# Heads 78 and 79 stored by GpSimd in four DMAs of 5, 4, 116 and 3 rows

## The chip, the cores and the metric

The kernel runs on one core of a Trainium2 chip. The metric is the device time of one execution in microseconds (us). The kernel before took 133.29, 133.81 and 133.81 us in three runs, a median of 133.81 us; a fourth run, the profiled one, took 133.37 us.

The core has a TensorE (PE) for matrix products, a VectorE (DVE), a ScalarE (ACT) and a GpSimd (POOL) for elementwise work, and a SyncE (SP) that only issues transfers. Transfers between the chip's main memory and the core's own memory are run by sixteen DMA engines. GpSimd, SyncE and ScalarE each have a queue of their own to them: q0, q1 and q10 in the profile.

## The reference

```python
B, H, S, D = 8, 12, 512, 64
mask[i, j] = 1 if j == i or j is an ancestor of i in the binary heap tree, else 0
scores = einsum('bhqd,bhkd->bhqk', Q, K) / sqrt(D) + (1 - mask) * (-1e9)
weights = softmax(scores, axis=-1)
out = einsum('bhqk,bhkd->bhqd', weights, V)        # float32
```

So there are 96 heads of 512 tokens with 64 numbers each. A token attends only to itself and to the nodes above it in the tree. The inputs are float32, 12.58 MB each, and so is the output.

## The kernel before, in words

**Layout.** The 96 heads are worked off in 48 pairs, `i = 0` to 47 (`NP` = 48). On the core a head of the output is a block of 128 partitions with 256 float32 numbers each: partition `p` holds tokens `4p` to `4p + 3`, which in main memory is one unbroken row of 1 KB. Eight heads share a tile `of` of 128 x 8 x 4 x 64 (`ofs[j]`, L695), from a pool of eleven, so that no tile of results has to be reused early.

**A pair.** `scores1` and `scores2` multiply queries and keys on TensorE and take the exponential on ScalarE; the mask enters as a second, short product. `values` (L650) multiplies the weights with V, with a column of ones that yields the sums; `norm` (L692) divides on VectorE, a reciprocal at L699 and a product at L701, and writes the head into `of`.

**Loads and stores.** All loads of Q, K and V but the first few are issued by GpSimd, in the order of one list that `pool_program` (L725) writes out by hand. The list also holds copies that GpSimd makes itself. `pool(i)` (L843) is called once per pair and takes operations from the head of the list as long as `ready` (L773) lets them; for a store that is `i >= 4 * (h0 // 8 + 1)`, when all heads of the tile have been issued to VectorE. Operations are never overtaken, so a DMA that waits on GpSimd holds back all that follow.

**The stores.** `store` (L708) writes `n` heads from `h0`, and partitions `p0` to `p1` of them, in one DMA. The main loop puts them on three queues:

- GpSimd (at the end of `pool_program`, L763 to L770) stores tiles of eight heads each, heads 0 to 71 and 80 to 87, a DMA of 1 MB each, and in between heads 74 to 79, a DMA of 768 KB. The last three entries of its list that move output are heads 64 to 71, 74 to 79 and 80 to 87.
- SyncE stores heads 72 and 73 in `store_apart` (L719), after pair 38: for each of the two heads one DMA of partitions 0 to 115 and one of partitions 116 to 127.
- SyncE also stores the heads of the last four pairs: 88 and 92 in one DMA, then 89, 93, 90, 94 and 91 in one of 128 KB each (L898 to L903); ScalarE issues head 95 (L904).

The GpSimd list ends with copies (`lay_beside`, L440) that rearrange the last tiles of queries and keys; two of them stand between heads 64 to 71 and heads 74 to 79.

**Semaphores.** The DMAs that GpSimd issues take eight semaphores in turn. A DMA whose semaphore is still that of an earlier one waits for the earlier one's landing before it is issued. Such waits are written by the framework and not in the kernel's text.

Of the kernel before, what the change touches and what calls it, by code (L numbers as in the profile page):

```python
# [119 lines left out]
def kernel(  # L120
# [7 lines left out]
    nc = tc.nc  # L128
    B, H, S, D = Q.shape
    P = nc.NUM_PARTITIONS  # L130
# [6 lines left out]
    KB, VB = 8, 16  # L137
# [577 lines left out]


    APART, APART_AT, APART_ROWS = 72, 38, 116

    def store_apart():  # L719

        for p0, p1 in ((0, APART_ROWS), (APART_ROWS, P)):
            for h in range(2):
                store(nc.sync, APART + h, 1, 1, p0, p1)

    def pool_program():  # L725

        ops = [
            (load_k, 2, 2), (load_q, 2, 2), (load_v, 0, 4), (load_v, 4, 4),
            (load_k, 4, 2), (load_k, 6, 2), (load_q, 4, 2), (load_k, 8, 4),
            (load_q, 6, 2), (load_q, 8, 4), (load_v, 8, 8), (load_k, 12, 4),  # L730
            (load_q, 12, 4), (load_k, 16, 4), (load_rows, 1, "upper"),
            (load_q, 16, 4), (load_rows, 1, "even"), (load_k, 20, 4), (load_rows, 1, "odd"),
            (load_q, 20, 4), (load_k, 24, 8), (load_q, 24, 4), (load_rows, 2, "upper"),
            (load_q, 28, 4), (load_rows, 2, "leaves0", "leaves1"), (load_k, 32, 8), (load_q, 32, 8),
            (load_rows, 3, "upper"),
            (spread_pool, (1, "Z0", 8, 16), (1, "Z1", 8, 16), (1, 6, 8, 16), (1, 9, 8, 16)),
            (load_q, 40, 8), (load_k, 40, 8), (load_rows, 3, "leaves0", "leaves1"), (load_q, 48, 8),
            (spread_top, 2), (spread_pool, (2, "Z0", 0, 16), (2, "Z1", 0, 16)), (load_k, 48, 8),
            (spread_pool, (2, "X", 0, 16), (2, "M", 0, 16), (2, "D1", 0, 16)), (spread_top, 3, 0, 12),
            (load_rows, 4, "upper"), (spread_top, 3, 12, 16),  # L740
        ]
        loaded, stored = 72, 0
        for h in range(56, NH, KB):
            top = [(spread_top, h // VB + 0)] if h % VB == 8 and 4 <= h // VB + 0 < NH // VB else []
            if top:
                top.append((spread_pool, (h // VB, "Z0", 0, 16), (h // VB, "Z1", 0, 16)))
            ops += [(load_q, h, KB)] + top + [(load_k, h, KB)]
            if h == 64:
                ops.append((
                    spread_pool, *[(3, part, 0, 16) for part in ("Z0", "Z1", "X", "M", "D1")]  # L750
                ))
            while loaded < min(h + 32, NH):
                names = ("leaves0", "leaves1") if loaded % VB else ("upper",)
                ops.append((load_rows, loaded // VB) + names)
                loaded += KB
            if top:
                o = h // VB
                ops.append((spread_pool, *[(o, part, 0, 16) for part in ("X", "M", "D1")]))
            if stored + KB + BEHIND <= h + KB:
                ops.append((store, nc.gpsimd, stored, KB))  # L760
                stored += KB
        ops.insert(-1, (lay_beside, "qst", 80 // KB))
        while stored < NH - KB:  # L763
            n = 2 if stored == APART else 0
            ops.append((store, nc.gpsimd, stored + n, KB - n))
            if stored == 40:
                ops.append((lay_beside, "kst", 80 // KB))
            if stored == 64:
                ops += [(lay_beside, "qst", 88 // KB), (lay_beside, "kst", 88 // KB)]
            stored += KB  # L770
        return ops
# [58 lines left out]
    def spread_by(copy, table, steady, i):  # L830
# [7 lines left out]
        for args in todo:  # L838
            spread(copy, *args)

    program = pool_program()

    def pool(i):  # L843
# [91 lines left out]
```

## Time and profile before

| | us |
|---|---|
| median of 3 runs | 133.81 |
| lowest and highest | 133.29, 133.81 |
| the profiled execution, its time | 133.37 |
| its span in the profile | 131.6 |
| granted TensorE clock, mean | 0.975 |

The span is from the first instruction to the last; what lies between the span and the time of the same execution, 1.8 us, is start and end of the program outside it. "Windows" are stretches of the span with the busy time of each engine in them, the granted clock, the share of time that the sixteen DMA engines were busy (1.00 is all sixteen, and a little over 1 occurs because packets overlap) and the bytes that they moved. The DMA view of a window has the same share in 40 slices, in tenths, the GB/s of each slice, and the packets of each queue (packets, MB, share). A timeline row has the start, the busy time, the engine, the line and the operation, and in brackets the idle time ahead of it and what ended it. "Landing" is the time from the issue of a DMA to the last of its semaphore's increments.

### The profile page before, as it was taken

The page shows a single profiled execution, that of the slowest core. Times are in us where ns is not written, and L with a number is a line of the kernel's source. Part 1 is how long each engine was busy: PE and PEld are TensorE (multiplying, and loading weights), DVE is VectorE, ACT ScalarE, POOL GpSimd, SP SyncE. Part 2 cuts the span into 40 slices and gives each one's busy share as a digit, 9 for nine tenths or more (in the row PEclk, how much of TensorE's full clock was granted, in tenths as well). Part 3 has the DMA queues.
Part 4 walks back from the last instruction along what each step waited for, and adds up shares of the span by engine and source line. Part 5 has one row for each costly group of instructions (what it writes and reads, how often), then busy time and mean ns, then how long its engine had stood idle before and what let it go on. Part 6 is the DMA issues. An engine that isn't in the chain of part 4 may idle for free.

```text
span 131.6 us, 5430 instructions
## 1 busy us (share of the span) xinstructions
PE 114.2 (87%) x2350; PEld 79.7 (61%) x2353; DVE 104.3 (79%) x254; ACT 101.1 (77%) x163; POOL 83.2 (63%) x114
## 2 busy tenths in 40 slices
PE   6985999999899897899999897896999999999800
PEld 2451676667567566677677674675676777666500
DVE  3528769988999998989899889898799977973620
ACT  4358289989799995968998788796799789899700
POOL 6988726245493999995399899944999945002000
PEclk9998599999999999999999999999999999999995
DMA  4999999999999999999999999999999999999992
GB/s 118 230 176 194 196 199 204 197 205 203 201 204 208 207 207 205 208 207 203 207 207 201 306 270 205 285 291 234 339 218 333 240 291 399 399 402 399 389 342 72
DMA packets 27959, 32.25 MB, mean 245 GB/s; under 512 B 1208, under 2 KB 23096, under 8 KB 27936
## 3 DMA queue, kind: packets, MB, share of 16 engines
q0 software_dynamic: 25760, 29.89, 111.4%
q1 hardware_dynamic: 1616, 1.57, 3.5%
q10 hardware_dynamic: 560, 0.46, 1.2%
q8 instruction: 18, 0.29, 0.8%
q14 instruction: 5, 0.04, 0.1%
HBM read 37.94 MB, written 12.58 MB: 384 GB/s over the span
## 4 chain that ended last, share of the span: by engine, by line
PE 34%; DVE 25%; DMA 16%; ACT 8%; POOL 7%; issue 5%; ACTq 0%; POOLq 0%
PE ob L662 12%; DMA kst<-in_K_dram 11%; DVE of L701 8%; DVE vt L371 6%; DMA qst<-in_Q_dram 5%; ACT e L618 4%; PE s L567 4%; POOL vt L371 3%; ACT e L584 3%; PE s L574 3%; DVE rec L699 2%; PE s L601 2%; PE ktp L477 2%; DVE kq L486 2%; PE s L612 2%
## 5 line engine op out<-in xcount | busy, mean ns | idle before, releaser
L584 ACT ACTIVATE e<-s 128x1024 bf16<-128x1024 f32 x40 | 40.9, 1022 | 13.0 <-PE s L574 12.5
L662 PE MATMUL ob<-vt,e 128*128 128x65 bf16 (+1 forms) x940 | 37.6, 198 | 1.6 <-DVE of L701 1.2
L662 PEld LDWEIGHTS <-e 128*128 128x128 bf16 (+1 forms) x960 | 30.5, 103 | 9.9 <-PE s L612 1.3
L371 POOL COPY vt<-vst 32x512 int32<-32x512 int32 (+4 forms) x44 | 32.5, 739 | 4.8 <-PE ob L662 2.6
L618 ACT ACTIVATE e<-s 128x384 bf16<-128x384 f32 x80 | 34.7, 491 | 0.0
L701 DVE TENSOR_TENSOR of<-ob,rec 128x512 f32<-128x512 f32 x47 | 32.5, 692 | 1.6
L371 DVE COPY vt<-vst 32x1024 bf16<-32x1024 bf16 (+5 forms) x47 | 22.0, 467 | 2.4 <-DMA vst<-in_V_dram 1.6
L699 DVE RECIPROCAL rec<-ob 128x8 f32<-128x8 f32 x47 | 9.6, 205 | 11.1 <-PE ob L662 9.7
L574 PE MATMUL s<-qq,kq 64*128 64x512 bf16 x80 | 15.3, 377 | 0.0
L709 POOL DMA_DIRECT2D out_dram<-of x11 | 9.8, 895 | 8.5 <-DVE of L701 8.0
L612 PE MATMUL s<-qq,kq 64*128 64x160 bf16 (+1 forms) x320 | 14.9, 208 | 0.1
L612 PEld LDWEIGHTS <-kq 64*128 64x128 bf16 x320 | 12.4, 94 | 4.2 <-issue 0.3
L601 PEld LDWEIGHTS <-codes 40*128 40x128 bf16 x80 | 6.4, 95 | 10.5 <-issue 4.9
L567 PE MATMUL s<-far,codes 40*128 40x512 bf16 x64 | 12.5, 386 | 0.1
L254 POOL DMA_DIRECT2D qst<-in_Q_dram x12 | 8.5, 704 | 5.6 <-DMA kst<-in_K_dram 2.9
L543 DVE COPY qq<-qtp 128x1024 bf16<-128x1024 bf16 x16 | 10.9, 683 | 1.0 <-PE qtp L538 1.0
L580 ACT ACTIVATE e<-s 128x1024 bf16<-128x1024 f32 x8 | 8.2, 1022 | 4.6 <-PE s L574 4.6
L371 ACT COPY vt<-vst 32x512 int32<-32x512 int32 (+3 forms) x19 | 10.4, 545 | 1.4 <-DMA vst<-in_V_dram 1.0
L601 PE MATMUL s<-far,codes 40*128 40x384 bf16 x64 | 10.6, 324 | 0.6 <-ACT e L618 0.5
L254 POOL DMA_DIRECT2D kst<-in_K_dram x11 | 8.5, 775 | 4.1 <-DMA vst<-in_V_dram 1.8
L477 PE MATMUL ktp<-ptile,kst 128*64 128x128 bf16 x256 | 9.9, 220 | 0.9 <-DMA kst<-in_K_dram 0.6
L538 PE MATMUL qtp<-ptile,qst 128*64 128x128 bf16 x192 | 7.4, 220 | 2.9 <-DMA qst<-in_Q_dram 2.0
(56 smaller groups left out, 155.3 us busy)
## 6 DMA issues: line engine op xcount, KB each, us to landing
out_dram<-of POOLq DMA_DIRECT2D x10, 1024.0 KB, 15.4
kst<-in_K_dram POOLq DMA_DIRECT2D x9, 512.0 KB, 14.3
qst<-in_Q_dram POOLq DMA_DIRECT2D x8, 512.0 KB, 16.2
vst<-in_V_dram POOLq DMA_DIRECT2D x12, 256.0 KB, 13.7
vst<-in_V_dram POOLq DMA_DIRECT2D x6, 512.0 KB, 12.7
qst<-in_Q_dram POOLq DMA_DIRECT2D x6, 256.0 KB, 12.4
kst<-in_K_dram POOLq DMA_DIRECT2D x4, 256.0 KB, 9.7
out_dram<-of POOLq DMA_DIRECT2D x1, 768.0 KB, 14.7
```

The costliest lines, as they stand in the source:

```text
L254: return nc.gpsimd.dma_start(out=kept[b][:, h0 % KB:h0 % KB + n, :, :].rearrange("p (g x) t d -> p g (x t d)", x=x), in_=src[:, h0 // x:(h ...
L371: return copy(out=dst, in_=src)
L477: nc.tensor.transpose(out=columns(kp[64 * a:64 * a + 64, :], mixed, *dims), in_=st[:, place[a], 4 * u + t, :], identity=ptile[:, 0:128],)
L567: nc.tensor.matmul(out=sp[:, a, :], lhsT=(k1code if i < WIDE else k1wide)[64 * a:64 * a + CODE_ROWS, :], rhs=(q1code, q1wide, q1far)[(i >= ...
L574: nc.tensor.matmul(out=sp[:, a, :], lhsT=keys(i, a, TOP), rhs=qTs[i][64 * a:64 * a + 64, :, :].rearrange("p t c -> p (t c)"), start=False, ...
L584: ) if i < WIDE else nc.scalar.activation(
L601: nc.tensor.matmul(out=flat[:, a, :, :].rearrange("p u (t c) -> p u t c", t=4)[:, :, :, 32 // n:], lhsT=k2wide[64 * a:64 * a + CODE_ROWS, ...
L612: nc.tensor.matmul(out=flat[:, a, :, lo:hi], lhsT=keys(i, a, WTILE2[t]), rhs=qT[64 * a:64 * a + 64, :, lo:hi], start=False, stop=t == 1, s ...
L618: nc.scalar.activation(out=e2s[i % NE][:, a, :, 32:128].rearrange("p t (r u) -> p t r u", u=n), in_=flat[:, a, :, :].rearrange("p u (t r) ...
L662: nc.tensor.matmul(out=ob[lo:hi, a, 65 * t:65 * t + 65], lhsT=e[:, a, PLACE[t], lo:hi], rhs=vt[vtile[tile_v][0]][:, head(i, a) % VB, vtile ...
L699: nc.vector.reciprocal(out=rec[:, a:a + n, :, :], in_=o4[:, a:a + n, :, D:D + 1])
L701: nc.vector.tensor_tensor(out=ofs[j][:, h0:h1 + 1:head(i, 1) - head(i, 0), :, :], in0=o4[:, a:a + n, :, 0:D], in1=rec[:, a:a + n, :, :].to ...
```

## The change

The list's entry for heads 74 to 79 becomes five entries: heads 74 to 77 over all partitions, and heads 78 and 79 over partitions 0 to 4, 5 to 8, 9 to 124 and 125 to 127. They stand at the same place of the list, ahead of heads 80 to 87. `store` and `ready` are as before, and so is everything on the other queues and engines.

```diff
     APART, APART_AT, APART_ROWS = 72, 38, 116
+    PIECES = ((0, 5), (5, 9), (9, 125), (125, P))
...
         while stored < NH - KB:
-            n = 2 if stored == APART else 0
-            ops.append((store, nc.gpsimd, stored + n, KB - n))
+            if stored == APART:
+                ops.append((store, nc.gpsimd, stored + 2, 4))
+                for p0, p1 in PIECES:
+                    ops.append((store, nc.gpsimd, stored + 6, 2, 1, p0, p1))
+            else:
+                ops.append((store, nc.gpsimd, stored, KB))
```

GpSimd's instructions grow from 84 to 88 rows in the built program, by four DMAs; the instructions of the other engines stand in the same order.

## The prediction

> **What bounds the kernel now.** I read the page's head and slices first, then the end of the span in windows, then the DMA view of single windows, then GpSimd's own timeline.
>
> ```profile
> span 131.6 us, 5430 instructions
> PE 114.2 (87%) x2350; PEld 79.7 (61%) x2353; DVE 104.3 (79%) x254; ACT 101.1 (77%) x163; POOL 83.2 (63%) x114
> DMA  4999999999999999999999999999999999999992
> ```
>
> No engine is full, while the sixteen DMA engines are busy in every slice but the first and the last. The end, in windows of 2 us and then of 0.5 us; the last two columns are the DMA share and GB/s:
>
> ```profile
> 118.00:120.00 2.00, 1.84 (x36) 1.20 (x37) 0.78 (x3) 2.00 (x5) 0.89 (x1) 1.00 1.02 400
> 120.00:122.00 2.00, 2.00 (x38) 1.22 (x35) 1.08 (x3) 1.83 (x5) 0.00 (x0) 1.00 1.02 404
> 122.00:124.00 2.00, 1.81 (x40) 1.21 (x36) 0.95 (x4) 1.97 (x5) 0.00 (x0) 1.00 1.02 391
> ...
> 126.00:126.50 0.50, 0.00 (x0) 0.00 (x0) 0.00 (x0) 0.00 (x0) 0.00 (x0) 1.00 0.92 338
> 126.50:127.00 0.50, 0.00 (x0) 0.00 (x0) 0.00 (x0) 0.00 (x0) 0.00 (x0) 1.00 1.07 391
> 127.00:127.50 0.50, 0.00 (x0) 0.00 (x0) 0.00 (x0) 0.00 (x0) 0.00 (x0) 1.00 0.95 340
> 127.50:128.00 0.50, 0.00 (x0) 0.00 (x0) 0.00 (x0) 0.00 (x0) 0.00 (x0) 1.00 0.86 299
> 128.00:128.50 0.50, 0.00 (x0) 0.00 (x0) 0.00 (x0) 0.00 (x0) 0.00 (x0) 0.98 0.72 248
> 128.50:129.00 0.50, 0.00 (x0) 0.00 (x0) 0.00 (x0) 0.00 (x0) 0.00 (x0) 0.50 0.54 189
> 129.00:129.50 0.50, 0.00 (x0) 0.00 (x0) 0.00 (x0) 0.00 (x0) 0.00 (x0) 0.50 0.34 117
> 129.50:130.00 0.50, 0.00 (x0) 0.00 (x0) 0.00 (x0) 0.00 (x0) 0.00 (x0) 0.50 0.19 66
> 130.00:130.50 0.50, 0.00 (x0) 0.00 (x0) 0.00 (x0) 0.00 (x0) 0.00 (x0) 0.50 0.04 14
> ```
>
> After 126.0 no engine computes and the queues still drain for over 4 us. The drain is not level: the share falls in steps from 127.5 to 130.5, as one DMA engine after another runs out of its part. From 126.0 on the shares add up to 0.5 x 5.63 = 2.8 us of all sixteen, so level queues would be empty at 128.8. The DMA view of the last 3.6 us, in 40 slices of 0.09 us, shows who is late:
>
> ```profile
> DMA  7777655565433333333100000000000000000000
> GB/s 251 273 273 262 216 205 194 182 216 182 148 125 125 114 114 114 114 114 103 57 34 23 23 23 23 11 0 0 0 0 0 0 0 0 0 0 0 0 0 0
> ```
>
> 23 GB/s is one engine, alone from 129.9 to 130.3. 114 is five, from 129.2 to 129.7. 273 at 128.1 is twelve: four had nothing left, 2.2 us before the last one. So what sets the end is the most loaded DMA engine; the chain of waits does not show this, since it ends with the last multiplication on VectorE. The rest of the span, 1.3 us, is the landing of the last write and the closing barrier. A kernel that moves the same bytes gains only by moving them from late engines to early ones.
>
> **The change part by part.** The bytes stay the same, as do the tiles and the order on the other engines. One store of six heads becomes one of four heads and four of two heads, over 5, 4, 116 and 3 partitions.
>
> *Price of a row.* At 398 GB/s (the windows of 118 to 124 lie between 391 and 404) an engine writes 24.9 GB/s: a head's row of 1 KB takes 41 ns, and heads 78 and 79 of one partition take 82 ns. With 128 rows on sixteen engines each has 8 of them, 0.66 us.
>
> *Where the rows go.* The kernel already stores heads 72 and 73 from SyncE, each in pieces of 116 and 12 rows, issued at 104.3 to 107.1. This window shows how they ran:
>
> ```profile
> DMA packets 477, 1.61 MB, mean 402 GB/s; under 512 B 25, under 2 KB 104, under 8 KB 477
> ...
> q0 software_dynamic: 393, 1.53, 96.7%
> q1 hardware_dynamic: 84, 0.08, 5.7%
> ```
>
> This is 112 to 116 us, when SyncE (q1) had nothing but these pieces under way. An engine with both queues takes turns: one packet of 4 KB (1.53 MB in 393 packets), 164 ns, then one of 1 KB, 41 ns, so some 4 / 0.205 = 19.5 of each in 4 us. 84 packets of q1 are then four engines' worth; sixteen would have moved about 310. So 116 rows went to four engines, 29 each, on SyncE's queue. If GpSimd's queue splits likewise, 5, 4, 116 and 3 rows go to 5 + 4 + 4 + 3 = 16 engines: twelve get one row instead of eight, and four get 29. A twelve-engine member loses 7 x 82 ns = 0.57 us, one of the four gains 21 x 82 ns = 1.72 us. The whole effect is which four. The Trainium skill (DMA: Bandwidth & Descriptors, "Why a DMA increments its semaphore by 16 and not by 1") says that a DMA uses the largest number of engines up to 16 that divides its outer dimension, which the 84 packets agree with, and that GpSimd's are consecutive engines from a cursor that goes round. By that page, a cursor at engine 0 would put the 116 rows on engines 9 to 12 and one at 3 on engines 12 to 15; no row here shows the cursor.
>
> *The sum in the likeliest case.* If the four are those that were idle at 128.1, they end by 128.1 + 1.72 = 129.8 at most (less, as they had gaps before). The last of the others goes from 130.3 to 130.3 - 0.57 = 129.75. So the end moves by -0.5 to -0.57 us. I take -0.55: 133.37 (span 131.6 and 1.8 around it) becomes 132.8. The profiled run is 0.44 below the median of 133.81 and near the lowest, 133.29; the mean of the four times is 133.6, and from there it is 133.0, which I forecast.
>
> *Five issues for one.* GpSimd around them:
>
> ```profile
> 109.25 1.04 POOL L445 COPY kst<-kst 128x1024 int32<-128x1024 int32 x1 [1.51 <-DMA kst<-in_K_dram]
> 110.74 0.84 POOL L709 DMA_DIRECT2D out_dram<-of  x1 [0.45 <-DVE of L701]
> 119.11 0.89 POOL L709 DMA_DIRECT2D out_dram<-of  x1 [7.53 <-DVE of L701]
> ...
> L290 POOL DMA_DIRECT2D vst<-in_V_dram x8 | 4.7, 596 | 2.5 <-DMA vst<-in_V_dram 1.5 <-DMA kst<-in_K_dram 0.6 <-DMA qst<-in_Q_dram 0.4
> ```
>
> The piecewise issues cost between 0.60 us (the loads of 32 partitions, the nearest row) and 0.89 us each. I take 0.6, as fewer descriptors: 0.84 + 4 x 0.6 = 3.2 us, at most 4.4, ending at 114 to 115.2. The idle 7.53 us ahead of the store of heads 80 to 87 hide all of it. Without that cover it would be 2.4 to 3.6 us late, and with it the rows that follow in GpSimd's queue.
>
> *Waits.* GpSimd's DMAs go round eight semaphores, and one that reuses a semaphore waits for the landing eight DMAs before. The 116-row piece now waits for the store issued at 100.15, the 3-row piece for that of 101.05, and the store of heads 80 to 87 for that of 102.92. Landing after issue for these three (least, middle, most):
>
> ```profile
> L709 POOL DMA_DIRECT2D out_dram<-of x3: 885/895/913, 100.1 to 102.9; - x3
> ...
> DMA to landing us min/median/max: 11.6/13.3/14.1
> ```
>
> So 111.8, 114.4 and 117.0 in that order. Behind the 3-row piece stands only the store of 80 to 87, whose data come at 119.1: 2.1 us of cover after the last of these waits. Cost zero. The queue doesn't run dry meanwhile: the store that was issued at 110.74 took 14.7 us to land, behind the five issued from 100.15 to 104.7.
>
> ```profile
> out_dram<-of POOLq DMA_DIRECT2D x1, 768.0 KB, 14.7
> ```
>
> One page speaks against the change: the Trainium skill (DMA: Bandwidth & Descriptors, "Rules for kernel authors") wants small transfers joined, as below 64 KB one pays mostly a fixed cost, which it puts at about 2.0 us. As an estimate by it, five transfers one after the other take 10 us from 110.74 and delay the store of 80 to 87 by 1.6 us; issues of 0.9 us beside landings of 11.6 us and more show that they are not one after the other here.
>
> **The rivals.**
> (a) *The four are late engines.* One mechanism: the order in which GpSimd's queue hands out engines is the only thing that picks the four, and no row of before shows it. If one of the five still busy after 129.2 is among them, it ends at 129.7 to 130.3 + 1.72 = 131.4 to 132.0, so 1.1 to 1.7 us later: 134.7 to 135.3, slower. It decides from the point where the chosen engine's old end plus 1.72 passes 130.3, which is an old end after 128.6. For it: only four of sixteen had ended by 128.1, so a blind choice hits late ones mostly. Against it: SyncE's pieces have already put 29 rows instead of 8 of each of two heads on four engines, 2 x 21 x 41 ns = 1.7 us more than on the others, so four of the five late ones are likely these; a choice that misses them can meet one late engine at most.
> (b) *The four lie in the middle*, with old ends of 128.6 to 129.2: 130.3 to 130.9, or 0 to 0.6 us later, 133.6 to 134.2. The same point decides; the falling shares from 0.54 to 0.34 are three or four engines that end there.
> (c) *The change doesn't do what it says:* GpSimd's queue deals 116 rows like 128, 8 to an engine. Then fifteen engines keep their load, the first few get up to 3 rows more (0.25 us) and the last one or two lose theirs (0.66 us); the end stays within -0.3 to +0.2 us of 130.3, the time at 133.3 to 133.8. The same section of the skill names such an exception for some direct copies. The 84 packets are of SyncE's queue and don't speak on GpSimd's.
> (d) *Something else sets the end*, as the last issue, too late for any levelling:
>
> ```profile
> 125.57 0.42 DVE L701 TENSOR_TENSOR of<-s,rec 128x256 f32<-128x256 f32 x1
> 126.03 0.35 ACTq L709 DMA_DIRECT2D out_dram<-of  x1
> ```
>
> From 126.38 the last 128 KB need 8 x 41 ns = 0.33 us per engine and a start of under 1.7 us (four engines had ended theirs by 128.1), so 128.1: it binds 1.6 us below where the change leaves the end. It takes nothing away.
>
> **How the numbers follow.** Likeliest case 0.45, (a) 0.18, (b) 0.18, (c) 0.13, others of either sign 0.06. Of 133.6, 0.5% (about what a measurement can tell) is 0.67 us, just more than the 0.55 forecast, so that case gives 0.23 to faster and 0.22 to same. (a) is slower, 0.18; (b) slower 0.11, same 0.07; (c) same 0.11, slower 0.02; others 0.03 to each of faster and slower. Together 0.26, 0.40, 0.34. The range begins at the lowest shown, 133.29, less 0.57 and a little, 132.5, and ends within (a), at 135.1; the likeliest case's own is 132.5 to 133.4.
>
> **What would show it right or wrong.** Right: the last slice with DMA traffic at 129.8 instead of 130.3, the share over 128 to 129 above the 0.63 that the two rows give, no 0.4 us at 23 GB/s. (a) or (b): four engines, 92 GB/s, alone at the end, for 1 us and more under (a). (c): the old steps, and an end within 0.3 us of the old. GpSimd's issues should be over by 115.2 and the store of 80 to 87 still issued at about 119.1 after VectorE; if it waits for a DMA instead, the semaphore count was wrong. The time of all compute before 126.0 should not move by more than 0.2 us; a shift there would make the whole reading wrong.

## The result, and the profile after

The change made the kernel slower: 133.67 us (median of 22 runs) against 133.17 us for the kernel before (22 runs beside it), a ratio of 1.0040 with a 95% interval of 1.0026 to 1.0054. That is 0.5 us: less than the 0.5% that the prediction set as its bound for "slower", yet no change (a ratio of 1) lies well outside the interval, and it is the other way than forecast.

The page of the changed kernel, its span and the packets (the kernel before had 27959, 1208 of them under 512 B):

```profile
span 131.8 us, 5438 instructions
DMA packets 28247, 32.25 MB, mean 245 GB/s; under 512 B 1488, under 2 KB 23376, under 8 KB 28224
L709 POOL DMA_DIRECT2D out_dram<-of x15 | 13.2, 884 | 6.9 <-DVE of L701 6.9
```

The third line is the group of GpSimd's stores: four more than the eleven of before, and no wait for a DMA ahead of any. The last windows of the changed kernel, with the DMA view from 128 us on (slices of 0.09 us):

```profile
127.50:128.00 0.50, 0.00 (x0) 0.00 (x0) 0.47 (x3) 0.00 (x0) 0.00 (x0) 1.00 0.87 309
128.00:128.50 0.50, 0.00 (x0) 0.00 (x0) 0.24 (x1) 0.00 (x0) 0.00 (x0) 1.00 0.96 336
128.50:129.00 0.50, 0.00 (x0) 0.00 (x0) 0.00 (x0) 0.00 (x0) 0.00 (x0) 1.00 0.93 322
129.00:129.50 0.50, 0.00 (x0) 0.00 (x0) 0.00 (x0) 0.00 (x0) 0.00 (x0) 1.00 1.02 357
129.50:130.00 0.50, 0.00 (x0) 0.00 (x0) 0.00 (x0) 0.00 (x0) 0.00 (x0) 0.91 0.44 148
130.00:130.50 0.50, 0.00 (x0) 0.00 (x0) 0.00 (x0) 0.00 (x0) 0.00 (x0) 0.50 0.22 78
130.50:131.00 0.50, 0.00 (x0) 0.00 (x0) 0.00 (x0) 0.00 (x0) 0.00 (x0) 0.50 0.02 6
```

```profile
DMA  9779999779998999954433333111000000000000
GB/s 376 251 250 387 376 387 319 250 273 376 375 387 296 353 398 364 308 171 148 148 114 114 114 114 103 57 46 46 23 0 0 0 0 0 0 0 0 0 0 0
```

VectorE still computes until 128.2 here, which before ended at 126.0. This is not the change: the TensorE clock was granted at half speed for 3.4 us in the middle of this execution, and the profile of before had its such stretch near 14 us, where less hung on it. The windows of the changed kernel:

```profile
88.00:92.00 4.00, 2.34 (x60) 1.69 (x60) 3.14 (x8) 2.75 (x6) 1.93 (x4) 1.00 1.17 226
92.00:96.00 4.00, 4.00 (x66) 2.80 (x66) 1.89 (x4) 2.28 (x4) 3.78 (x6) 0.57 1.09 325
96.00:100.00 4.00, 4.00 (x100) 2.96 (x98) 3.90 (x9) 3.10 (x6) 2.96 (x4) 1.00 1.18 238
```

All computing behind it is 2.2 us late, and yet the last DMA traffic ends at 130.6 instead of 130.3. So the DMA engines set the end here too, though the late computing is not far behind: the store that ScalarE issues last, at 128.27, is landed by eleven of the sixteen engines at 129.82 to 130.13, and by the last at 130.93. The prediction had named a shift of the computing as a sign against its whole reading; the version with a piece of 9 rows, below, has the same loss without the shift. The drain is not level in the changed kernel either; five engines (114 GB/s) are busy until 130.2 and two (46) until 130.5.

Where the 116 rows went is seen in the sixteen increments of each DMA's semaphore, one from each DMA engine. They are in the trace, here in us, sorted, for three of the five DMAs of the changed kernel (the pieces of 5 and of 3 rows are left out):

```
heads 74-77  120.69 120.76 120.96 122.59 122.80 122.97 122.98 123.21 123.28 123.31 123.76 123.83 124.05 124.23 124.29 124.95
4 rows       121.02 121.17 121.30 122.97 123.20 123.34 123.35 123.60 123.66 123.79 124.13 124.24 124.42 124.55 124.65 125.31
116 rows     121.20 121.38 121.48 123.17 123.41 124.14 124.31 124.46 124.61 124.72 124.85 125.33 125.34 125.49 125.65 125.67
```

Three engines are 1.6 us ahead of all others, a fourth leads the rest. From the 4 rows to the 116 the first five move on by 0.18 to 0.21 us. 29 rows take 2.4 us by the prediction's price of a row, so none of these five has them. Behind 123.41 there is a gap: the engines that stood at 123.34 and 123.35 are gone from there, and the last five increments of the 116 rows fall close together, 2 us on. The four engines are from the middle of the field.

The increments tell the order of the engines better than their working time, since an increment lands some time after the packet that writes it: on the first engine, 0.35 us lie between the packet that ends heads 74 to 77 and the one that ends the 3-row piece (120.22 to 120.57), and 0.68 us between the first increments of the two DMAs (120.69 to 121.37).

### The profile page after: what moved, and what is told of

Same layout as the page of the kernel before. It is cut to its first block, busy times and chain, and to the rows that moved or that the text cites. A ratio compares the mean times of both kernels' runs of the same rounds, so it can differ in the third digit from the quotient of the medians.

```text
span 131.8 us, 5438 instructions
## 1 busy us (share of the span) xinstructions
PE 116.5 (88%) x2353; PEld 80.3 (61%) x2353; DVE 104.9 (80%) x254; ACT 101.1 (77%) x163; POOL 86.9 (66%) x118
## 4 chain that ended last, share of the span: by engine, by line
PE 34%; DMA 26%; POOL 14%; DVE 10%; ACT 8%; issue 5%; ACTq 0%; POOLq 0%
DMA qst<-in_Q_dram 14%; POOL vt L371 11%; PE ob L662 9%; DMA vst<-in_V_dram 8%; PE s L567 5%; DMA firstQ<-in_Q_dram 4%; DVE of L701 4%; PE s L574 4%; ACT e L618 3%; ACT e L584 2%; PE qtp L409 2%; DVE vt L371 2%; PE s L601 2%; PE s L612 2%; PE ktp L470 1%
## 5 line engine op out<-in xcount | busy, mean ns | idle before, releaser
L371 DVE COPY vt<-vst 32x1024 bf16<-32x1024 bf16 (+5 forms) x47 | 22.9, 486 | 0.9
L709 POOL DMA_DIRECT2D out_dram<-of x15 | 13.2, 884 | 6.9 <-DVE of L701 6.9
```

Source lines behind the costliest of these rows:

```text
L371: return copy(out=dst, in_=src)
L709: return eng.dma_start(out=Or[p0:p1, h0:h0 + step * (n - 1) + 1:step, :], in_=ofs[h0 // 8][p0:p1, h0 % 8:h0 % 8 + step * (n - 1) + 1:step, ...
```

## The experiments

All of them change the row `PIECES` alone, so heads 74 to 77 still go in one DMA, and 78 and 79 in the pieces shown. Every time stands beside runs of the kernel before on the same chip (133.2 to 133.3 us), five rounds each. "Place" counts DMA engines in the order in which GpSimd's queue deals them out, place 0 being the first engine of the first piece; a piece of 12 rows moves the deal on by twelve places, one of 32 or 48 rows uses all sixteen and leaves it where it was.

**Four DMAs, rows level.**

```diff
-    PIECES = ((0, 5), (5, 9), (9, 125), (125, P))
+    PIECES = ((0, 32), (32, 64), (64, 96), (96, P))
```

> Heads 78 and 79 in four DMAs of 32 rows each: as many DMAs, issues and semaphore waits as in the change, but every DMA engine keeps 8 rows. Theory A (place: the 29 rows per engine went to engines that were not early, the number of DMAs costs little): level with the kernel before, 133.2 within 0.2 us. Theory B (count: each added DMA costs every DMA engine and GpSimd something, whatever its rows): as slow as the change, 133.5 to 133.8 us.

133.38 us, ratio 1.0008 (0.9988 to 1.0028): level. This carries the same number of issues, of semaphores and of waits as the change, so none of these is its loss.

**The 116 rows turned by three places forward, to the front, and the change with one piece fewer.**

```diff
+    PIECES = ((0, 12), (12, P))                      # places 12 to 15
+    PIECES = ((0, 116), (116, P))                    # places 0 to 3
+    PIECES = ((0, 9), (9, 125), (125, P))            # places 9 to 12, as the change
```

> Heads 78 and 79 in two DMAs, 12 rows and then 116: twelve engines' worth of single rows are dealt out before the 116 rows instead of nine. Theory A: the 116 rows move on by three engines; if those are the four that ended first, 132.6 to 132.9 us; if they are late ones, 134 us and more; in any case not the 133.67 us of the change. Theory B: two added DMAs fewer than the change, so halfway between, 133.4 us, with the same engines late as in the change.

> The same two DMAs in the other order, 116 rows first. Theory A: the 116 rows fall on the first four engines in the order of dealing; if these are the ones that SyncE's pieces of heads 72 and 73 already load, the end comes 1.1 to 1.7 us later, 134.3 to 134.9 us. Theory B: as with 12 rows first, 133.4 us.

> The pieces of 5 and 4 rows joined to one of 9: the 116 rows begin after as many engines as in the change, with one DMA fewer. Theory A: as the change, 133.67 within 0.2 us. Theory B: a quarter of the loss less, 133.5 us.

134.90 (1.0132, 1.0103 to 1.0161), 134.68 (1.0113, 1.0089 to 1.0138) and 133.89 us (1.0048, 1.0020 to 1.0076). By the medians, the same 116 rows cost 0.5 to 0.6 us or 1.4 to 1.6 us, depending on nothing but the rows dealt before them, and 9 rows in one piece are as good as 5 and 4. So the place decides and not the count. The end of the two slow ones in the DMA view, 128 to 132.6 us in slices of 0.115 us, first with 12 rows ahead:

```profile
DMA  9975523222321212121221221111110000000000
GB/s 365 330 267 196 196 98 134 107 107 98 116 98 54 89 62 80 53 80 62 71 80 62 71 80 62 45 54 36 53 45 18 27 0 0 0 0 0 0 0 0
```

and with the 116 rows first:

```profile
DMA  8999997444333323333333221000000000000000
GB/s 303 419 347 383 365 374 241 143 178 160 116 143 107 134 98 125 116 116 125 116 116 107 80 80 62 27 27 18 27 27 18 27 0 0 0 0 0 0 0 0
```

In the first, four engines' worth of traffic (98 to 107 GB/s) is left alone at 128.6, three of them go on to 130.8 and one or two to 131.6. In the second five are left from 129.2 to 130.4. The last issue on ScalarE is late in both profiles, at 126.59 and 127.19 instead of 126.03, but eleven of the sixteen increments of that store are in by 128.96 and 129.67, and the last come at 131.56 and 131.93: again the engines set the end. With 116 rows first the four are late ones in any reading; I had expected these to be the engines that SyncE's pieces load, and the size fits (1.1 to 1.7 us expected, 1.4 measured), but which engines those are was not shown by a run of its own.

The piece of 9 gives the change without the late stretch of half clock: its last issue on ScalarE is at 125.98, as before (126.03). Its DMA view, in the same slices:

```profile
DMA  9997859997655433322311100000000000000000
GB/s 356 330 401 267 312 187 365 392 339 241 232 187 178 151 125 134 116 80 98 107 62 62 53 9 0 0 0 0 0 0 0 0 0 0 0 0 0 0 0 0
```

Three to five engines (80 to 134 GB/s) are left from 129.6 to 130.3, and the last write ends at 130.7 instead of 130.3. This is the picture that the prediction named for the rivals (a) and (b).

**The places between.**

```diff
+    PIECES = ((0, 4), (4, 120), (120, P))            # places 4 to 7
+    PIECES = ((0, 5), (5, 121), (121, P))            # places 5 to 8
+    PIECES = ((0, 6), (6, 122), (122, P))            # places 6 to 9
+    PIECES = ((0, 7), (7, 123), (123, P))            # places 7 to 10
```

> Pieces of 4, 116 and 8 rows: the 116 rows begin 4 engines after the start of the dealing. In the trace of the change, of the four engines that ran dry first one had its row from the 5-row piece, two from the 4-row piece and one from the 3-row piece, none from the 116. Theory A (a fixed order of dealing, the same start in every run): places 4 to 7 then hold the one of the 5-row piece and one or two of the 4-row piece, and the last engine is relieved: 132.8 to 133.4 us unless the remaining one or two are late (then 133.8). Theory C (the dealing starts elsewhere in each kernel): no relation to the traces so far, 133.7 to 134.9 us like the others.

> Pieces of 5, 116 and 7 rows, places 5 to 8, exactly those that had the 4-row piece in the change. Theory A: two of the four are early ones, the other two are middle or late: 133.2 to 134 us. Theory C: unrelated, 133.7 to 134.9 us.

> Pieces of 6, 116 and 6 rows, places 6 to 9. Theory A: at least one early engine and one of those of the change: 133.4 to 134 us. Theory C: unrelated, 133.7 to 134.9 us.

> Pieces of 7, 116 and 5 rows, places 7 to 10, two of them those of the change. Theory A: 133.5 to 134 us, near the 133.67 us of the change. Theory C: unrelated, 133.7 to 134.9 us.

Ratios 1.0056 (1.0035 to 1.0077), 1.0047 (1.0028 to 1.0067), 1.0033 (1.0016 to 1.0051) and 1.0044 (1.0022 to 1.0065). None gains. The expectation for 4 to 7 was missed (133.99 us against 132.8 to 133.4, or 133.8 with late engines among the four); the other three times (133.91, 133.78 and 133.85) lie where they were expected. All four also lie in the 133.7 to 134.9 us of theory C, so the times alone don't tell the two theories apart. The increments do, as they show whom the 116 rows hit; for 5 to 8, for example:

```
5 rows       120.77 120.82 121.19 122.76 123.24 123.29 123.30 123.37 123.41 123.43 123.77 123.99 124.07 124.09 124.91 125.06
116 rows     121.37 123.01 123.02 123.03 123.47 123.54 123.59 123.62 124.04 124.18 124.38 125.19 125.23 125.36 125.44 126.24
```

Of the three early ones one stays (121.19 to 121.37), two join the field 2.2 us later, and the fourth (122.76) moves by 0.27 only. Read in this way, the seven windows give:

| places of the 116 rows | of the first three engines, hit | the fourth hit | ratio |
|---|---|---|---|
| 0 to 3 | 0 | no | 1.0113 |
| 4 to 7 | 1 | yes | 1.0056 |
| 5 to 8 | 2 | no | 1.0047 |
| 6 to 9 | 2 | no | 1.0033 |
| 7 to 10 | 2 | no | 1.0044 |
| 9 to 12 (the change; 9 rows in one piece) | 0 | no | 1.0040; 1.0048 |
| 12 to 15 | 1 | no | 1.0132 |

One set of places agrees with all rows: the first three are at 7, at 8 and at one of 13 to 15, the fourth at 4. They are not four neighbours, so no version with 116 rows could hit these four alone. That one set fits all rows also speaks for a deal that begins at the same engine in every one of these kernels; the trace does not name the engines.

**Few engines with many rows, and fewer rows each.**

```diff
+    PIECES = ((0, 6), (6, 88), (88, 96), (96, P))    # 41 rows each at places 6 and 7
+    PIECES = ((0, 10), (10, 92), (92, 96), (96, P))  # 41 rows each at places 10 and 11
+    PIECES = ((0, 4), (4, 72), (72, 80), (80, P))    # 17 rows each at places 4 to 7
```

> As many pieces as in the change, of 6, 82, 8 and 32 rows: 82 rows are dealt to two engines, 41 each, at places 6 and 7 of the order. By the traces of the pieces 4-116-8, 5-116-7 and 6-116-6 these two ran dry first. All other engines keep 3 rows of 8. Theory A (the place decides): the others lose 5 rows of 82 ns, 0.41 us, less 0.15 us for fillers of the 82-row piece; the two early ones take 2.9 us more and still end before the last: 0.2 to 0.3 us below the kernel before, 133.0 us. If the number of DMAs or the unevenness itself costs the time: 133.7 us or more, and with 2.9 us on a late engine 135 us.

> The same with 10, 82, 4 and 32 rows: the same 41 rows on two engines, now at places 10 and 11, which had the 116-row piece in the change and end in the middle. Theory A: they end 2.9 us later than before, at 131.3 to 132.2 instead of 128.5 to 129.4, so the end comes 1.0 to 1.6 us later: 134.3 to 134.9 us. If the place doesn't matter: as with the early two, within 0.2 us.

> Pieces of 4, 68, 8 and 48 rows: four engines at places 4 to 7 (three early, one middle) with 17 + 3 rows, all others with 4. Theory A: 12 rows more are 0.98 us for the one middle engine, which then ends at 129.5 to 130.4, and 4 rows less are 0.33 us for the others: between 133.0 and 133.4 us, below the 133.99 us of 29 rows at the same places. If the place doesn't matter: 133.7 us.

134.87 (1.0116, 1.0095 to 1.0138), 134.55 (1.0105, 1.0068 to 1.0143) and 133.24 us (0.9999, 0.9978 to 1.0019). The second and third came as expected, the first did not: when I wrote it I took 6 and 7 for the early places. Its increments show one of the first three hit and one engine of the field that then ended alone. Its DMA view, same slices, has that engine (18 to 27 GB/s) alone from 130.6 to 131.8:

```profile
DMA  9986779997455999433111100000000000000000
GB/s 321 339 303 214 249 249 347 365 392 267 160 205 196 365 374 321 143 134 107 53 53 45 45 27 18 27 27 18 27 27 18 27 27 0 0 0 0 0 0 0
```

**The same sizes, one place on.**

```diff
+    PIECES = ((0, 7), (7, 89), (89, 96), (96, P))    # 41 rows each at places 7 and 8
```

> Pieces of 7, 82, 7 and 32 rows: the two engines with 41 rows are now those at places 7 and 8. Read anew, the landings of the pieces say that places 7 and 8 are two of the three engines that run dry first: the 116 rows hit one of the three at places 4 to 7 and at 12 to 15, two at 5 to 8, 6 to 9 and 7 to 10, none at 0 to 3 and 9 to 12; with 82 rows on places 6 and 7 one early engine got 41 rows and one middle engine, which then ended alone and last. Theory A: all other engines lose 0.41 us less 0.15 us for fillers, so 132.9 to 133.2 us, at or just below the kernel before, and 1.7 us below the same sizes at places 6 and 7 (134.87). If the size of the piece and not the place made that one slow: 134.5 to 135 us again.

133.43 us, 1.0024 (1.0000 to 1.0048): 1.4 us less than one place before, with as many pieces and the same 41 rows on each of two engines. The DMA view, same slices, ends at 130.4:

```profile
DMA  9998887764453211110000000000000000000000
GB/s 365 383 365 285 312 303 258 258 241 160 160 187 134 98 62 45 45 36 18 27 18 0 0 0 0 0 0 0 0 0 0 0 0 0 0 0 0 0 0 0
```

So the places 7 and 8 can take 41 rows each and are not last, as read from the windows. The expected gain of 0.1 to 0.3 us did not show, though. By the packets, the early engine with 3 rows here needs 1.88 us from the end of the store before heads 74 to 77 to the end of the pieces (118.79 to 120.67), 1.29 of it for the eight packets of heads 74 to 77. So the pieces take 0.59 us, 0.07 us less than the 0.66 of 8 rows; another engine, whose single row is dealt ahead of the 82, takes 0.42. A relief of 0.07 to 0.24 us is no more than the ends of single profiles differ (130.08 for the level pieces, 130.32 for the kernel before, where each engine writes the same). Why the ratio lies at or above 1 and not just below was not settled. No version tried beats the kernel before.

## Why the prediction was wrong

*What bounds the kernel: right.* Shown by the drains of the slower versions, in which a few engines work on alone while the others are done, and by the profile of the changed kernel, where all computing is 2.2 us late and the last traffic 0.3 us, no later than in the version with the piece of 9, whose computing is not late (130.6 and 130.7).

*116 rows go to four engines on GpSimd's queue as on SyncE's: right.* 16 semaphore writes for each of four more DMAs are 64 packets. The level pieces add just these, 1272 packets under 512 B instead of 1208. The change adds 280. The other 216 are tiny packets on the engines that a piece leaves out, 8 or 16 bytes each:

```
q0 packets by size      4 B    8 B   16 B
before                  992      0      0
after                  1056     48    168
```

48 are one for each engine left out of a piece: 11, 12, 12 and 13 engines, so the pieces used 5, 4, 4 and 3. The 168 are 14 for each of the twelve left out of the 116 rows. The rival (c) is out. This is what the Trainium skill (DMA: Bandwidth & Descriptors, "Why a DMA increments its semaphore by 16 and not by 1") says of 5, 4, 116 and 3 rows, and the windows agree with its engines in a row from a cursor.

*The relief of the twelve: right in kind, too large.* Predicted 0.57 us. By the trace, an engine with a single row needs 1.512 us from the end of the store before to the end of the 3-row piece, of which heads 74 to 77 take 1.288, so 0.22 us for heads 78 and 79 instead of 0.66: a relief of 0.44 us. That is so for two of the three early engines, whose row is dealt ahead of the 116; the third, whose row follows them, needs 0.34 us, since its packet takes 198 ns and not 84. (Two ahead and one behind is also what places 7, 8 and one of 13 to 15 ask for.) The term that was missing is 17 tiny packets, 15 for the 116 rows and one for each of two other pieces, and four added semaphore writes: 21 packets, about 7 ns from one to the next, are 0.15 us.

*"If the four are those that were idle at 128.1": this is the step that failed.* It was the whole forecast, and no row of before carried it, as the prediction said itself. The drain showed that four engines were early and that four get 29 rows, and I took the one four for the other at 0.45. The early ones stand at places 4, 7, 8 and one of 13 to 15, so no deal of four in a row can hit them all; the change hits 9 to 12, four of the middle. That is rival (b), which had 0.18: old ends plus 1.72, 133.6 to 134.2 us, and 133.67 measured. The old ends can be read from the increments of ScalarE's store in the kernel before:

```
head 95      127.63 127.64 127.75 128.19 128.48 128.74 128.80 128.95 129.24 129.25 129.38 130.03 130.05 130.11 130.15 130.68
```

Three early engines, a fourth, seven in the middle and five late ones. The last increment is 0.35 us behind the last packet (130.32); with this for all, the middle seven ended at 128.1 to 129.0, and with 1.72 more they end, as an estimate, at 129.8 to 130.7. The last packet ended at 130.60 in the changed kernel and at 130.72 with the piece of 9, and not at the 129.8 of the forecast case. Which of the seven were hit was not followed up to the end. The base was off as well: four runs gave 133.6 us, and the 22 give 133.17, from which the forecast case would be 132.6 and not 133.0. That the time lies inside the stated range of 132.5 to 135.1 us is owed to the rivals that the range took in, and not to the forecast case, which ended at 133.4.

*Rival (a) was priced right*, 1.1 to 1.7 us: with the 116 rows at places 0 to 3 and 12 to 15 it came to 1.4 and 1.6 us. It only was not the change's case. Its reason for the late engines, SyncE's pieces, remains unproven.

*Five issues for one, and the waits: cost nothing, as said.* The issues took 0.76, 0.60, 0.60, 1.28 and 0.57 us; the 116 rows cost more than the upper end of 0.89, and it didn't matter. The timeline of GpSimd in the changed kernel:

```profile
112.98 3.78 POOL L709 DMA_DIRECT2D out_dram<-of  x5 [2.33 <-DVE of L701]
121.35 0.93 POOL L709 DMA_DIRECT2D out_dram<-of  x1 [4.58 <-DVE of L701]
```

4.6 us of idle time remained ahead of heads 80 to 87, and it ended with VectorE and not with a DMA. In the level pieces, whose computing is not late, the last piece waited 1.6 us for a DMA and was issued at 114.61 (the prediction had 114.4), at a ratio of 1.0008, so this was covered too.

## What to carry to other kernels

Where sixteen DMA engines end unevenly, the drain tells how many are early but not which; before work is moved between them, find their places, by the sixteen increments of each DMA's semaphore or by turning the deal, and check that they are reachable together. A DMA of a row count that sixteen doesn't divide is a strong lever on a single engine: here the same 232 KB cost 0.5 to 1.6 us depending on a handful of rows ahead of it. Keep such pieces small for what is to be gained: at places 4 to 7, the time was level with 17 rows on each engine and not with 29.

## What the runs showed that I had not expected

Tiny packets go to the engines that a DMA leaves out, in proportion to the rows of the engines that it uses: 15 per engine for 29 rows of two heads. That they run on these engines is read from their count (168 is 14 for each of twelve).

SyncE's own issues become slow in some of the versions. Its last six stores, with the least, the middle and the longest issue in ns and the first and last start, in the kernel before and then in the kernel with the piece of 9 rows:

```profile
L709 SPq DMA_DIRECT2D out_dram<-of x6: 333/404/1117, 121.0 to 125.6; - x6
```

```profile
L709 SPq DMA_DIRECT2D out_dram<-of x6: 405/1044/1448, 120.9 to 127.6; - x6
```

The last store is issued 2 us later, with the data at the same time. It doesn't set the end: ten of its sixteen increments are in by 129.82, and the last comes at 131.07. Unevenness of the queues is not the explanation by itself. The level pieces have slow issues too:

```profile
L709 SPq DMA_DIRECT2D out_dram<-of x6: 361/640/1118, 120.8 to 126.5; - x6
```

And the slowest version, 12 rows and then 116, has a middle of 433 ns, near the 404 of the kernel before. What slows them was not tried and stays open, and so does whether it has to do with the gain that the 41 rows on early engines did not bring.
